# Low halves of 18 weight blocks by adding transfers, and three moves in the order of work, in a decoder layer

## The chip, the cores and the metric

The kernel runs on one core of a Trainium2 chip, as one launch. The metric is device time in microseconds, a median over runs. The core has a matrix engine (PE, with PEld for its weight loads), a vector engine (DVE), an activation engine (ACT), a general engine (POOL), and SyncE (SP), which only issues transfers. Each engine runs its own list of instructions in order and waits on semaphores. ACT and DVE can read the matrix engine's accumulators. Transfers (DMAs) are issued by SP, and by POOL where a transfer adds to what lies at its destination.

## The reference, cut to what matters

One layer of a hybrid decoder, width 1024, 512 tokens, all in float32:

```python
u = rmsnorm(h)
a_glu, q, k, v, r, g_low, gate_a, gate_b = split(u @ w_in)
c = conv31(a_glu[:, :1024] * sigmoid(a_glu[:, 1024:]))
y_conv = silu(layernorm(c)) @ w_conv_out
y_gla = (headnorm(gla_chunked(q, k, v, g_low)) * silu(r)) @ w_gla_out
h = h + (sigmoid(gate_a) * y_conv + sigmoid(gate_b) * y_gla) @ w_o
z = conv3(rmsnorm(h) @ w_ffn_up)            # 1024 -> 2 x 2816
h = h + (silu(z[:, :2816]) * z[:, 2816:]) @ w_ffn_down
return rmsnorm(h)
```

The change touches the layer norm of the convolution branch, the gates, and the channel mixer (`w_ffn_up`, called the up projection, and the product that follows it).

## The kernel before, in words

**Three matmuls for one.** A float32 product is made from parts: every operand is split into a high part, the value rounded to a shorter format, and a low part, what the rounding left over. `mm3` (L444 to L450) then issues three matmuls for one product: low times high, high times low, high times high. In `col_tile` the weight is the stationary operand; its 128x1024 block gives one tile of 128 output channels for 512 tokens, which are 8 x 3 matmuls of 512 columns. The first of each three (L448) reads the weight's low part, so a block can't begin before its low part is there.

**Getting a weight block.** The list `order` holds all blocks in the order of use. `load` lets SP fetch the next 512 KB block into one of four `raw` buffers; `split_weight` (L343 to L392) makes its two parts in one of four `whi` and one of four `wlo` buffers: ACT copies the block into the rounded format (L385), and DVE subtracts that copy from the block (L390). `weight` (used at the start of each block) calls `split_weight` two blocks ahead (`LOOK = 2`). Blocks named in the set `ADDED` (L43) go another way: ACT writes the negated, rounded copy into the low buffer (L387), and then POOL issues a transfer that fetches the block from memory a second time and adds it there (L388). DVE has no part in it. Before the change 16 blocks do so: six of `w_glu`, two of `w_v`, eight of `w_r`.

**Seven products for eight.** Some pairs of output tiles are made together by `two_tiles` with seven quarter products in place of eight (Winograd's form). Such a pair takes two raw blocks and a third buffer for sums that POOL makes of them (`two_sums`, L327): three additions at step `x1` and one at `x3`. The steps `x1`, `x3`, `x2`, `x4` use 256-column matmuls. `put` (L1171) copies an accumulator out on ACT, and `combine` (L1174) works on DVE; the step `x3` adds into the accumulator that `put` has to copy first.

**The merge.** `pair_7` runs such pairs for the gates, with half tiles of `w_gla` or `w_conv` behind each of the four steps. After the last step of a pair ACT takes the sigmoid of both tiles (L1255). Between the blocks, `fill` hands out pieces of side chains by shares: `norm_chain` (L897) is the layer norm of the convolution. Its `ln_center` squares the eight channel tiles and DVE adds the squares (L866); `ln_var` (L868) calls `token_sums` (L834), where PE sums over channels with one-column matmuls (L837); POOL takes the root, and `spread` (L844) brings it back. The order of instructions on each engine is set when the program is built, by a planner that works with costs of its own; `tc.keep_in_program_order` and `tc.issue_after` bind it.

**The up projection.** `up_plan` lists the work of three groups of channel tiles (`GROUPS`). Channel tile f has two blocks, f and 22 + f (`FT + f`). Plain tiles (f = 0, 2, 1, 3, 4, 5, 8 in the first group, 9, 20, 12 in the second, 13, 16, 17, 19 in the third) are `col_tile` blocks; the others are made in sevens. From the second half of the first group on, a unit weaves one plain tile (blocks a and b) into the steps of one pair, in one of three kinds:

- "opens" (tiles 9 and 13): a, x1, a, x3, b, x2, b, x4, b
- the middle kind (tiles 5, 20, 16, 17): x1, a, x3, a, x2, b, x4, b
- "closes" (tiles 8 and 12): x1, a, x3, a, x2, a, x4, and then all of b

`ffn_conv` (L1472) works on a finished tile: one ACT instruction (L1475) and two taps on DVE (L1477). `value` adds the silu (L1482). `second_of_pair` (L1508) makes the operands for the down projection; at L1647 it may be held behind the split of an `x3`. The down projection (`seven`) follows each group; its blocks are also completed by transfers that POOL issues (L317, L300).

Of the kernel before, what the change touches and what calls it, by code (L numbers as in the profile page):

```python
# [15 lines left out]
ALU = mybir.AluOpType  # L16

P = 128
D = 1024
T = 512  # L20
# [8 lines left out]
FT = FF // P  # L29
# [14 lines left out]
ADDED = {("w_glu", 2 * k) for k in range(2, KT)} | {("w_r", m) for m in range(KT)}  # L44
ADDED |= {("w_v", KT // 2 + j) for j in (0, 1)}
RATE = 5.0
WARM = (7, 3, 2)
MID = 4
EARLY = 2
PADS = (416, 2016, 768)  # L50
# [25 lines left out]
def trunk_layer(ctx: ExitStack, tc: tile.TileContext, a: dict, out: bass.AP):  # L76
    nc = tc.nc
# [26 lines left out]
    def heap(dt=F32):  # L104
        return hp.tile([P, T], dt, tag="h", name=nm("h"))
# [13 lines left out]
    def mm_bank():  # L119
        return ps.tile([P, T], F32, tag="mm", name=nm("mm"), bufs=5)  # L120

    def ax_bank():
        return ps.tile([P, T], F32, tag="ax", name=nm("ax"), bufs=3)
# [10 lines left out]
    ones = cp.tile([P, P], F32, name="ones")  # L134
# [264 lines left out]
    def third_ahead():  # L399

        n = used[0] + LOOK
        if n == len(ready) < len(order) and order[n][0] == "two" and order[n][1][-1] == "x3":
            split_weight()
            return two_low[0]
# [59 lines left out]
    def row_half(name, j0, n, acts, nk, done, tok_inner, middle=None):  # L464
# [19 lines left out]
        else:  # L484
            ws = [weight(name, j0 + k, 0) for k in range(nk // 2)]
            for t in range(NT):
                acc = mm_bank()
                for k in range(nk):
                    if middle and k == MID:
                        middle(t)  # L490
# [61 lines left out]
    start = tc.manual_schedule(engines=START)  # L552
# [13 lines left out]
    def warm(n):  # L566
        for _ in range(n):
            nc.tensor.matmul(idle[:, :P], ones, ones, start=True, stop=True)
# [3 lines left out]
    def transposed(x, g):  # L572
        tr = ax_bank()
        for k in range(4):
            c = (g * 4 + k) * P
            nc.tensor.transpose(tr[:, k * P : (k + 1) * P], x[:, c : c + P], ident)
        return tr
# [31 lines left out]
    def early_gain(t, g):  # L609
        xg[t, g] = with_gain(xg[t, g], g)  # L610
        eu[t, g] = [by_four(heap(F32R)) for _ in range(2)]
# [43 lines left out]
    def by_parts(acc, t, ks, parts=(HH, HL, LH)):  # L655

        for wi, ai in parts:
            for k in ks:
                act = eu[t, k // 4][ai][:, k % 4, :] if t < EARLY else acts1[k][ai][:, t * P : (t + 1) * P]
                j = slice((k % 2) * T, (k % 2 + 1) * T)  # L660
                first, last = k == 0 and (wi, ai) == HH, k == KT - 1 and (wi, ai) == LH
                nc.tensor.matmul(acc, act, ready[k // 2][wi][:, j], start=first, stop=last)  # L662

    accs = [mm_bank() for _ in range(EARLY)]
    warm(WARM[0])
    xg[0, 0] = transposed(xs[0], 0)
# [9 lines left out]
    highs[1]()  # L676
    warm(WARM[1])
    lows[0]()
# [5 lines left out]
    by_parts(accs[0], 0, (0, 1), (HL, LH))  # L684
    warm(WARM[2])
    early_gain(1, 0)
# [41 lines left out]
    acc = mm_bank()  # L728
# [7 lines left out]
    acc = mm_bank()  # L736
# [74 lines left out]
    for k in range(KT):  # L811
# [4 lines left out]
        c = heap()  # L816
# [17 lines left out]
    def token_sums(s):  # L834
        b = ax_bank()
        for t in range(NT):
            nc.tensor.matmul(b[:, t : t + 1], s[:, t * P : (t + 1) * P], ones[:, 0:1], start=True, stop=True)  # L837
        return b[:, :NT]

    def spread(v):  # L840
# [18 lines left out]
    def ln_center(k):  # L859
        nc.vector.tensor_tensor(conv[k], stat["mean"], conv[k], ALU.add)  # L860
        sq = btmp()
        nc.scalar.activation(sq, conv[k], AF.Square)
        if k == 0:
            stat["sq"] = sq
        else:
            nc.vector.tensor_tensor(stat["sq"], stat["sq"], sq, ALU.add)  # L866
# [30 lines left out]
    def norm_chain():  # L897
        chain = [(RATE, ln_parts)]
        chain.append((0, ln_mean))
        chain.extend((2, lambda k=k: ln_center(k)) for k in range(KT))  # L900
        chain[-1] = (RATE, chain[-1][1])
        chain.append((2.5, lambda: None))
        chain.append((RATE, ln_var))
        chain.append((2.5, lambda: None))
        chain.append((0, ln_rstd))
        chain.extend((2.5, lambda k=k: ln_out(k)) for k in range(KT))
        return chain
# [17 lines left out]
    for k in range(KT):  # L925
        s = slice(k * P, (k + 1) * P)
# [323 lines left out]
    part = [None] * KT  # L1250
    gas = {}

    def sigmoid(m, acc):
        g = heap()
        nc.scalar.activation(g, acc, AF.Sigmoid)  # L1255
        return g
# [25 lines left out]
    half_of = [range(KT // 2), range(KT // 2, KT)]  # L1282
    open_tiles = {}

    def pair_7(n):
        (name, p, q), behind = MERGE[n], BEHIND[n]
        unit = two_tiles(name, p, q, lambda: merge_acts, mm_bank)
        if behind[0][0] == "w_conv":
            while chains:
                fill(1)  # L1290
        for j in range(4):
            while urgent and j and len(urgent) > (5 if j == 1 else 0):
                urgent.pop(0)[1]()
            done = next(unit)
            if j == 3:
                third_ahead()
                for m, c in zip((p, q), done):
                    (part if name == "w_gb" else gas)[m] = sigmoid(m, c)
            for proj, m, half in behind[j : j + 1]:
                open_tiles[proj, m] = tile_of(proj, m, half_of[half], open_tiles.get((proj, m)))  # L1300

# [170 lines left out]
    def ffn_conv(acc, m):  # L1472
        z = tmp()
        w = [pp[:, PP_FW + m * FW + j : PP_FW + m * FW + j + 1] for j in range(FW)]
        nc.scalar.activation(z, acc, AF.Identity, bias=pp[:, PP_FB + m : PP_FB + m + 1], scale=w[2])  # L1475
        for j, s in ((1, 1), (0, 2)):
            nc.vector.scalar_tensor_tensor(z[:, s:], acc[:, : T - s], w[j], z[:, s:], ALU.mult, ALU.add)  # L1477
        return z

    def value(i, acc):  # L1480
        za = ffn_conv(acc, i)
# [113 lines left out]

    gain3 = None
    banks, values, units = {}, {}, {}
    third = None
    for gi, pairs in enumerate(GROUPS):
        acts = []  # L1600
        if gi == 0:

            ws = [weight("w_up", j, 0) for i in pairs[0] for j in (i, FT + i)]
            accs = [mm_bank() for _ in ws]
            for j, lo in [(j, lo) for lo in (0, H) for j in range(3)]:
                late = {(1, 0): (KT - 1, 2), (2, 0): (MID, 3)}.get((j, lo))
                at = {late[0]: lambda t=late[1]: to_channels(normed[t], u2, t)} if late else {}
                col_tile(ws[j], acts2, accs[j], lo, lo + H, at)
            col_tile(ws[3], acts2, accs[3])
            p, q = pairs[0]  # L1610
            w = first_gated(p, value(p, accs[0]), accs[1])
            found = first_of_pair(w)
            up_acts, sums = ffn_sums()
            s1_n2, of_s1, s4, of_n2, of_s4, n3, of_n3 = sums
            sums = [s1_n2, of_n2 + of_s1, s4 + n3, of_n3 + of_s4]

            def some_sums():
                for _, work in sums.pop(0) if sums else ():
                    work()

            some_sums()
            acts.append(second_of_pair(q, value(q, accs[2]), accs[3], w, found))
            some_sums()
        else:
            found = first_of_pair(w)
        for what, i, *rest in up_plan(gi):
            if what == "tile":
                if 0 in rest[0]:
                    banks[i] = (weight("w_up", i), mm_bank())
                wt, acc = banks[i]  # L1630
                col_tile(wt, acts2, acc, ks=rest[0])
                if KT - 1 in rest[0] and i < FT:
                    values[i] = value(i, acc)
            if what == "part":
                if rest[0] == "x1":
                    units[i] = two_tiles("w_up", i, FT + i, lambda: up_acts, ax_bank)
                done = next(units[i])
                if done:
                    values[i] = value(i, done[0])
                    banks[FT + i] = (None, done[1])  # L1640
                    third = third_ahead()
            if what == "first":
                w = first_gated(i, values.pop(i), banks.pop(FT + i)[1])
                if any(i in pair for pair in pairs):
                    found = first_of_pair(w)
            if what == "second":
                with tc.issue_after(third.ins) if third else ExitStack():  # L1647
                    acts.append(second_of_pair(i, values.pop(i), banks.pop(FT + i)[1], w, found))
                third = None
            if what in ("first", "second"):  # L1650
                some_sums()
        if gi < len(GROUPS) - 1:
            seven("w_down", pairs, acts, lambda t, n, c: None)
        else:
            gain3 = load_gain("final_g")
            seven("w_down", pairs, acts, last_complete, last_at, True)
# [90 lines left out]
```

## Time and profile before

| | before |
|---|---|
| median of 3 runs | 831.78 us (830.68 to 832.02) |
| profiled execution, its own time | 834.48 us |
| its span, first to last instruction | 832.8 us |
| granted clock of PE, mean | 0.993 |
| PE busy | 819.7 us |
| DVE busy | 717.5 us |
| ACT busy | 450.1 us |
| POOL busy | 149.4 us |

Rows of the timeline read: start, duration, engine, line, operation, output <- inputs, shape, count, and in brackets the engine's idle time before it and what ended it. Rows of the waits read: engine, tile and line that waited, what it waited for, total, times, longest. Rows of the windows: the stretch, its length, busy time of PE, PEld, DVE, ACT and POOL with counts, PE's granted clock, the share of the DMA engines, GB/s. Matmuls overlap, so a row's duration is longer than the distance to the next one. A DMA issue's "us to landing" runs from its issue to the last byte's semaphore.

### The profile page before, as it was taken

The page shows a single profiled execution, that of the slowest core. Times are in us where ns is not written, and L with a number is a line of the kernel's source. Part 1 is how long each engine was busy: PE and PEld are TensorE (multiplying, and loading weights), DVE is VectorE, ACT ScalarE, POOL GpSimd, SP SyncE. Part 2 cuts the span into 40 slices and gives each one's busy share as a digit, 9 for nine tenths or more (in the row PEclk, how much of TensorE's full clock was granted, in tenths as well). Part 3 has the DMA queues.
Part 4 walks back from the last instruction along what each step waited for, and adds up shares of the span by engine and source line. Part 5 has one row for each costly group of instructions (what it writes and reads, how often), then busy time and mean ns, then how long its engine had stood idle before and what let it go on. Part 6 is the DMA issues. An engine that isn't in the chain of part 4 may idle for free.

```text
span 832.8 us, 11561 instructions
## 1 busy us (share of the span) xinstructions
PE 819.7 (98%) x4325; PEld 707.6 (85%) x4325; DVE 717.5 (86%) x1161; ACT 450.1 (54%) x666; POOL 149.4 (18%) x133
## 2 busy tenths in 40 slices
PE   8999999999999999899999999999999999999996
PEld 6888888888888889889988898899889988899885
DVE  5689999998989599685778889979984999789996
ACT  5744447656563446494444546556444664456654
POOL 1000010001100213335000200221133301513012
PEclk9999999999999999899999999999999999999999
DMA  7355672563433113223458633046743356324762
GB/s 289 112 123 149 151 185 98 128 152 101 105 100 109 43 50 103 92 87 102 160 144 228 177 102 102 26 136 172 145 130 102 130 146 141 129 84 157 189 128 102
DMA packets 30616, 106.27 MB, mean 128 GB/s; under 512 B 3464, under 2 KB 3600, under 8 KB 30560
## 3 DMA queue, kind: packets, MB, share of 16 engines
q1 hardware_dynamic: 24800, 85.35, 30.4%
q0 software_dynamic: 5760, 20.19, 14.5%
q8 instruction: 34, 0.56, 0.3%
q14 instruction: 22, 0.18, 0.1%
HBM read 103.42 MB, written 2.10 MB: 127 GB/s over the span
## 4 chain that ended last, share of the span: by engine, by line
PE 87%; DVE 8%; issue 2%; ACT 1%; DMA 1%; SPq 0%; POOL 0%; POOLq 0%; ACTq 0%; DVEq 0%
PE mm L448 25%; PE mm L449 25%; PE mm L450 25%; PE ax L450 2%; PE ax L448 2%; PE ax L449 2%; PE mm L662 2%; DVE wlo L356 1%; DMA pp<-in_pp_dram 1%; PE ax L1062 1%; DVE btmp L866 1%; DVE tmpq L1129 1%; DVE wlo L390 1%; PE ax L1064 1%; PE ax L1043 1%
## 5 line engine op out<-in xcount | busy, mean ns | idle before, releaser
L448 PE MATMUL mm<-uh,wlo 128*128 128x512 f32 (+1 forms) x672 | 244.5, 364 | 0.0
L449 PE MATMUL mm<-ul,whi 128*128 128x512 f32 (+1 forms) x672 | 242.3, 361 | 0.0
L450 PE MATMUL mm<-uh,whi 128*128 128x512 f32 (+1 forms) x672 | 241.9, 360 | 0.0
L450 PEld LDWEIGHTS mm<-uh,whi 128*128 128x128 f32 x672 | 126.7, 189 | 19.4
L448 PEld LDWEIGHTS mm<-uh,wlo 128*128 128x128 f32 x672 | 127.0, 189 | 19.1 <-DVE tmp L1174 0.2
L449 PEld LDWEIGHTS mm<-ul,whi 128*128 128x128 f32 x672 | 127.0, 189 | 18.7
L385 ACT CAST whi<-raw 128x1024 fp32r<-128x1024 f32 x86 | 89.6, 1046 | 61.6 <-PE mm L450 38.7
L356 DVE TENSOR_TENSOR wlo<-raw,whi 128x1024 fp32r<-128x1024 f32 x80 | 96.9, 1217 | 27.2 <-ACT whi L355 23.0
L327 POOL TENSOR_TENSOR raw<-raw,raw 128x512 f32<-128x512 f32 x42 | 68.2, 1623 | 222.6 <-DVE wlo L356 127.8
L390 DVE TENSOR_TENSOR wlo<-raw,whi 128x1024 fp32r<-128x1024 f32 x70 | 89.1, 1277 | 16.2 <-ACT whi L385 16.0
L355 ACT CAST whi<-raw 128x1024 fp32r<-128x1024 f32 x80 | 76.3, 958 | 37.6 <-PE mm L450 27.9
L783 DVE SCALAR_TENSOR_TENSOR c<-h,pp,c 128x255 f32<-128x255 f32 (+14 forms) x120 | 57.2, 477 | 3.6 <-ACT c L779 3.3
L783 DVE SCALAR_TENSOR_TENSOR c<-aside,btmp,c 128x255 f32<-128x255 f32 (+14 forms) x120 | 57.2, 477 | 2.8 <-ACT c L779 2.7
L783 DVE SCALAR_TENSOR_TENSOR aside<-h,pp,aside 128x255 f32<-128x255 f32 (+6 forms) x112 | 53.4, 477 | 0.0
L355 ACT CAST whi<-kept 128x1024 fp32r<-128x1024 f32 (+1 forms) x32 | 31.8, 996 | 31.1 <-DVE kept L310 14.8
L1477 DVE SCALAR_TENSOR_TENSOR tmp<-mm,pp,tmp 128x511 f32<-128x511 f32 (+1 forms) x56 | 41.5, 744 | 4.0 <-ACT tmp L1475 3.9
L356 DVE TENSOR_TENSOR wlo<-kept,whi 128x1024 fp32r<-128x1024 f32 (+1 forms) x32 | 37.9, 1186 | 4.3 <-ACT whi L355 4.3
L1171 ACT COPY tmp<-mm 128x256 f32<-128x256 f32 x48 | 17.7, 368 | 34.0 <-PE mm L450 33.5
L1394 DVE TENSOR_TENSOR hres<-hres,mm 128x512 f32<-128x512 f32 (+1 forms) x49 | 32.4, 672 | 3.3 <-PE mm L450 2.0
L1475 ACT ACTIVATE tmp<-mm,pp 128x512 f32<-128x512 f32 x28 | 21.7, 774 | 18.8 <-PE mm L450 18.6
L387 ACT ACTIVATE wlo<-raw 128x1024 fp32r<-128x1024 f32 x16 | 16.8, 1059 | 22.1 <-PE mm L448 22.1
L1477 DVE SCALAR_TENSOR_TENSOR tmp<-tmp,pp,tmp 128x511 f32<-128x511 f32 (+1 forms) x32 | 27.1, 905 | 0.1
(350 smaller groups left out, 1792.3 us busy)
## 6 DMA issues: line engine op xcount, KB each, us to landing
raw<-in_w_up_dram SPq DMA_DIRECT2D x44, 512.0 KB, 3.5
raw<-in_w_glu_dram SPq DMA_DIRECT2D x16, 512.0 KB, 4.8
raw<-in_w_down_dram SPq DMA_DIRECT2D x15, 512.0 KB, 3.9
kept<-in_w_down_dram POOLq DMA_DIRECT2D x10, 512.0 KB, 6.5
raw<-in_w_v_dram SPq DMA_DIRECT2D x8, 512.0 KB, 5.7
raw<-in_w_qk_dram SPq DMA_DIRECT2D x8, 512.0 KB, 3.4
raw<-in_w_r_dram SPq DMA_DIRECT2D x8, 512.0 KB, 4.5
wlo<-in_w_r_dram POOLq DMA_DIRECT2D x8, 512.0 KB, 8.0
```

What stands on the lines that cost most here:

```text
L327: work = nc.gpsimd.tensor_tensor(out, x, y, ALU.add)
L355: nc.scalar.copy(hi, raw)
L356: two_low[:] = [nc.vector.tensor_tensor(lo, raw, hi.bitcast(F32), ALU.subtract)]
L385: nc.scalar.copy(hi, raw)
L390: pace[0] = nc.vector.tensor_tensor(lo, raw, hi.bitcast(F32), ALU.subtract)
L448: nc.tensor.matmul(acc, ll, rh, start=first, stop=False, **kw)
L449: nc.tensor.matmul(acc, lh, rl, start=False, stop=False, **kw)
L450: nc.tensor.matmul(acc, lh, rh, start=False, stop=last, **kw)
L783: nc.vector.scalar_tensor_tensor(out[:, j:], x[:, : half_t - j], w, out[:, j:], ALU.mult, ALU.add)
L1394: done = nc.vector.tensor_tensor(hres[t, n][:, c], hres[t, n][:, c], acc[:, c], op)
L1475: nc.scalar.activation(z, acc, AF.Identity, bias=pp[:, PP_FB + m : PP_FB + m + 1], scale=w[2])
L1477: nc.vector.scalar_tensor_tensor(z[:, s:], acc[:, : T - s], w[j], z[:, s:], ALU.mult, ALU.add)
```

## The change

Four things are changed. (1) The set `ADDED` gets both blocks of the tiles 1, 3, 4, 5, 8, 20, 12, 16 and 17 of the up projection, 18 blocks: for each, the subtraction on DVE is replaced by a negated copy on ACT and an adding transfer on POOL's queue. (2) The token sums keep their place in the program's order, and the chain's shares are changed so that `ln_var` comes later: on PE the eight passes of L837 move behind a half step of the pair and a half tile of `w_gla`, 30 matmuls. (3) In `pair_7` the sigmoids of the first three pairs are taken only after the next pair's first step. (4) `second_of_pair` is also held behind the last tap of `value`, so that both taps of the value tile come ahead of the other tile's.

```diff
+ADDED |= {("w_up", m) for f in (1, 3, 4, 5, 8, 20, 12, 16, 17) for m in (f, FT + f)}
...
-            nc.tensor.matmul(b[:, t : t + 1], s[:, t * P : (t + 1) * P], ones[:, 0:1], start=True, stop=True)
+            product = nc.tensor.matmul(b[:, t : t + 1], s[:, t * P : (t + 1) * P], ones[:, 0:1], start=True, stop=True)
+            tc.keep_in_program_order(product)
...
         chain.extend((2, lambda k=k: ln_center(k)) for k in range(KT))
-        chain[-1] = (RATE, chain[-1][1])
-        chain.append((2.5, lambda: None))
+        chain += [(2.5, lambda: None)] * 4
         chain.append((RATE, ln_var))
...
+    complete_pairs = []
+
     def pair_7(n):
...
             done = next(unit)
+            if j == 0 or n >= 3:
+
+                while complete_pairs:
+                    complete_pairs.pop(0)()
             if j == 3:
                 third_ahead()
-                for m, c in zip((p, q), done):
-                    (part if name == "w_gb" else gas)[m] = sigmoid(m, c)
+
+                def sigmoids(done=done):
+                    for m, c in zip((p, q), done):
+                        (part if name == "w_gb" else gas)[m] = sigmoid(m, c)
+
+                complete_pairs.append(sigmoids)
+                if n >= 3:
+                    complete_pairs.pop()()
...
         for j, s in ((1, 1), (0, 2)):
-            nc.vector.scalar_tensor_tensor(z[:, s:], acc[:, : T - s], w[j], z[:, s:], ALU.mult, ALU.add)
+            taps_at[:] = [
+                nc.vector.scalar_tensor_tensor(z[:, s:], acc[:, : T - s], w[j], z[:, s:], ALU.mult, ALU.add)
+            ]
...
-    third = None
+    third = []
...
-                    third = third_ahead()
+                    third = [taps_at[0], third_ahead()]
...
-                with tc.issue_after(third.ins) if third else ExitStack():
+                with ExitStack() as order_of:
+                    for ins in third:
+                        if ins:
+                            order_of.enter_context(tc.issue_after(ins.ins))
                     acts.append(second_of_pair(i, values.pop(i), banks.pop(FT + i)[1], w, found))
-                third = None
+                third = []
```

More of the change, by code (lines that the diff above doesn't have):

```diff
@@ L1476, in ffn_conv @@
         for j, s in ((1, 1), (0, 2)):
-            nc.vector.scalar_tensor_tensor(z[:, s:], acc[:, : T - s], w[j], z[:, s:], ALU.mult, ALU.add)
+            taps_at[:] = [
+                nc.vector.scalar_tensor_tensor(z[:, s:], acc[:, : T - s], w[j], z[:, s:], ALU.mult, ALU.add)
+            ]
         return z
+    taps_at = []
     def value(i, acc):
```

## The prediction

> **What bounds the kernel now.** I read the page's sums first, then the chain, PE's waits and windows, and at last the single rows around each edit.
>
> ```profile
> span 832.8 us, 11561 instructions
> PE 819.7 (98%) x4325; PEld 707.6 (85%) x4325; DVE 717.5 (86%) x1161; ACT 450.1 (54%) x666; POOL 149.4 (18%) x133
> PE 87%; DVE 8%; issue 2%; ACT 1%; DMA 1%; SPq 0%; POOL 0%; POOLq 0%; ACTq 0%; DVEq 0%
> 490.00:580.00 90.00, 90.00 (x531) 80.04 (x529) 82.81 (x107) 51.94 (x73) 13.38 (x9) 1.00 0.32 101
> 620.00:680.00 60.00, 59.47 (x381) 53.92 (x380) 47.66 (x63) 33.01 (x49) 15.55 (x10) 1.00 0.35 116
> 713.00:775.00 62.00, 62.00 (x393) 56.30 (x392) 50.47 (x66) 34.17 (x51) 19.45 (x11) 1.00 0.40 136
> ```
>
> The matrix engine is the bound: 98% busy, 87% of the chain. The last three rows are windows over the three groups of the up projection, where the 18 blocks lie: PE is busy for 90.00 of 90, 59.47 of 60 and 62.00 of 62 us, at a granted clock of 1.00. So relief of DVE can win next to nothing there, and each microsecond for which a block's low part is late is lost whole. What the change can win lies at PE's few stops:
>
> ```profile
> PE ax L837 <- DVE btmp L866: 2.1, 1, 2.1
> PE mm L448 <- ACT tmp L1171: 1.1, 2, 0.6
> 334.36 0.28 PE L450 MATMUL mm<-sumsq,whi 128*128 128x256 f32 x1
> 336.73 1.50 PE L837 MATMUL ax<-ones,btmp 128*128 128x1 f32 x8 [2.10 <-DVE btmp L866]
> 338.09 0.56 PE L448 MATMUL mm<-sumsq,wlo 128*128 128x256 f32 x1
> 337.00:344.00 7.00, 7.00 (x30) 6.61 (x30) 1.62 (x4) 1.04 (x1) 2.91 (x3) 0.51 0.01 2
> 372.68 0.39 PE L448 MATMUL mm<-xq,wlo 128*128 128x256 f32 x1 [0.55 <-ACT tmp L1171]
> 668.90 0.39 PE L448 MATMUL mm<-xq,wlo 128*128 128x256 f32 x1 [0.53 <-ACT tmp L1171]
> ```
>
> PE waits 2.10 us for the last square (L866), does its eight thin passes, and then runs 7 us at a granted clock of 0.51; two waits of half a microsecond follow.
>
> **Token sums.** Thirty matmuls go ahead of L837. At 0.12 us for a 256-column one (334.36 against its neighbours) and 0.23 for a 512-column one, a half step of the pair (18) and a half tile (12) make 4.9 us. PE comes to L837 at about 339.2, and the squares were there by 336.6: the wait goes, 2.10 us. With it goes the stretch from 334.6 to 338.1 without large matmuls, after which the clock was halved; 7.0 x (1 - 0.51) = 3.4 us more. Next on this chain is `spread` (L844):
>
> ```profile
> 338.26 0.16 DVE L870 TENSOR_SCALAR mean<-ax 128x4 f32<-128x4 f32 x1 [1.68 <-PE ax L837]
> 338.90 1.01 POOL L500 TENSOR_TENSOR rstd<-mean,mhalf 128x4 f32<-128x4 f32 x1
> 350.01 1.05 PE L844 MATMUL ax<-ident,rstd 128*128 128x128 f32 x8
> ```
>
> It stands at 350.01 with no wait, and moved up by the 5.5 us it comes at 344.5. The passes, begun at 339.2, take 1.4 us (336.73 to 338.09), and the root is done 1.8 us behind them (338.90 + 1.01), at 342.4: still not late, by 2 us. Gain 5.5.
>
> **Sigmoids and taps.** The sigmoids of a pair go behind the next pair's first step, so the copy (L1171) that PE waits for at 372.68 stands ahead of them on ACT: I take 0.5 of the 0.55. For the taps, the 0.53 at 668.90 could go as well, but a11's copy is also put behind new work of ACT (below); I count nothing. Bounds 0 and 1.1. Gains together 6.0 us.
>
> **The 18 blocks.** Each takes one subtraction from DVE and adds one negation on ACT, one issue on POOL and 512 KB of traffic:
>
> ```profile
> L390 DVE TENSOR_TENSOR wlo<-raw,whi 128x1024 fp32r<-128x1024 f32 x70 | 89.1, 1277 | 16.2 <-ACT whi L385 16.0
> L387 ACT ACTIVATE wlo<-raw 128x1024 fp32r<-128x1024 f32 x16 | 16.8, 1059 | 22.1 <-PE mm L448 22.1
> L388 POOL DMA_DIRECT2D wlo<-in_w_r_dram x8: 844/870/924, 147.8 to 237.0; - x8
> DMA to landing us min/median/max: 5.4/7.9/10.9
> 56.76 1.07 ACT L387 ACTIVATE wlo<-raw 128x1024 fp32r<-128x1024 f32 x1 [3.45 <-PE mm L448]
> 58.13 0.87 POOL L388 DMA_DIRECT2D wlo<-in_w_glu_dram  x1 [9.82 <-ACT wlo L387]
> 58.41 0.80 SPq L257 DMA_DIRECT2D raw<-in_w_glu_dram  x2
> raw<-in_w_up_dram SPq DMA_DIRECT2D x44, 512.0 KB, 3.5
> ```
>
> DVE loses 18 x 1.28 = 23 us, ACT gains 18 x 1.06 = 19 us (10 blocks in the first window: 51.9 to 62.5 of 90), POOL 18 x 0.87 = 16 us. None of the three is full, so by load this costs nothing. The price is the time until the low part is there. Before, it was one subtraction behind the copy. Now it is the negation, 1.06, the step to POOL's issue (56.76 + 1.07 to 58.13, 0.30), and the landing, for which I take L388's median 7.9: together 9.3 us, with 6.8 and 12.3 by its least and greatest. I take the median, as the next raw load is issued within a microsecond of the adding one (58.41 behind 58.13), and that will be so again: the negation frees the raw buffer.
>
> In the Trainium skill, "DMA: Bandwidth & Descriptors", section "Anatomy of one DMA — SWDGE (gpsimd) path", a transfer issued by POOL is fitted as 2.0 us plus its bytes over 436 GB/s. By that 512 KB would land after 3.2 us, an estimate, with no stall left at the tight blocks and a sum of 825.8; the least of L388's landings, 5.4, is well over it, so the trace doesn't agree.
>
> Most of the 18 have the time: the blocks of tiles 1, 3, 4, 5 and a8 are split two whole blocks ahead, more than 9.3 us before their use (3 by little: 0 to 0.9), and b20, b16, b17, b5 have steps of a pair between. The tight ones, with the copy's start and the first matmul that reads the low part (a and b are a tile's two blocks):
>
> ```profile
> 571.57 1.05 ACT L385 CAST whi<-raw 128x1024 fp32r<-128x1024 f32 x1
> 577.70 0.40 PE L448 MATMUL mm<-uh,wlo 128*128 128x512 f32 x1
> 638.25 1.05 ACT L385 CAST whi<-raw 128x1024 fp32r<-128x1024 f32 x1 [3.75 <-PE ax L450]
> 645.13 0.40 PE L448 MATMUL mm<-uh,wlo 128*128 128x512 f32 x1
> 673.55 1.05 ACT L385 CAST whi<-raw 128x1024 fp32r<-128x1024 f32 x1
> 679.62 0.40 PE L448 MATMUL mm<-uh,wlo 128*128 128x512 f32 x1
> 730.68 1.05 ACT L385 CAST whi<-raw 128x1024 fp32r<-128x1024 f32 x1 [3.75 <-PE ax L450]
> 737.56 0.40 PE L448 MATMUL mm<-uh,wlo 128*128 128x512 f32 x1
> 746.55 1.22 DVE L390 TENSOR_TENSOR wlo<-raw,whi 128x1024 fp32r<-128x1024 f32 x1
> 748.28 0.75 DVE L1477 SCALAR_TENSOR_TENSOR tmp<-mm,pp,tmp 128x511 f32<-128x511 f32 x1
> 748.94 0.69 DVE L356 TENSOR_TENSOR wlo<-raw,whi 128x512 fp32r<-128x512 f32 x1
> 749.76 3.53 POOL L327 TENSOR_TENSOR raw<-raw,raw 128x512 f32<-128x512 f32 x2 [11.86 <-DVE wlo L356]
> 753.26 2.27 POOL L327 TENSOR_TENSOR raw<-raw 128x512 f32<-128x512 f32 x1
> 758.58 0.40 PE L448 MATMUL mm<-uh,wlo 128*128 128x512 f32 x1
> ```
>
> - b8: its negation is put behind the copy, so 571.57 + 1.05 + 9.3 = 581.9 against 577.70: PE stops for 4.2 us (1.7 by the least landing, 7.2 by the greatest).
> - b12, the same place in the second group: 673.55 + 10.3 = 683.9 against 679.62, 4.2 (1.7 to 7.2). What a12 loses (as a17, below) is within this: the copy waits on work of DVE that runs on meanwhile.
> - a20 and a16: the buffer comes free only when PE has left it (3.75 us of waiting before the copy), and the negation stands ahead of the copy: 638.25 + 9.3 = 647.5 against 645.13, 2.4 (0 to 5.4); likewise 730.68 against 737.56, 2.4. The copies of accumulators behind them on ACT come some 2 us later; these stalls hide that, and it costs 1.2 each without them.
> - a17: its issue stands on POOL behind three sums that end at 755.5. They wait on DVE for x4's low part (748.94), which comes some 1.9 us earlier, as b16's subtraction (746.55, 1.22) and a tap (748.28, 0.75) are no longer ahead of it. Issue at 753.6, landing at 759.0 to 761.5, against 758.58: 1.6 (0.4 to 2.9).
>
> Stalls: 2 x 4.2 + 2 x 2.4 + 1.6 = 14.8 us.
>
> **The clock.** A stretch of some 3.5 us without large matmuls (334.6 to 338.1) halved the clock for 7 us; waits of 0.55 us didn't. A stall of 4.2 us is longer than that stretch, one of 2.4 shorter. I charge 3.4 us once, for b8; b12's 4.2 is split by a12. The Trainium skill, "TensorE: Matmul & The Clock Gate", "Part 1: The HAM clock gate", says the clock falls after an idle window of about 3.4 us that runs freely; by it 4.2 may trip and 2.4 can't, the sum taken here. Had the bare wait of 2.10 us done it, each of the four stalls would pay, which is the first rival. The trace alone doesn't part the two, as the wait and the thin passes adjoin.
>
> **Sum.** 14.8 + 3.4 - 6.0 = +12.2 us. The profiled execution took 834.48 us itself (832.8 of span and 1.7 around it), 2.7 above the median of the runs, 831.78; it becomes 846.7, and the median 844.0.
>
> **Rivals.**
> 1. Every stall of 2.1 us or more halves the clock: b12, a20 and a16 pay too, 3 x 3.4 = 10.2 more: 854.2. For it: the dip at 337 began right behind a wait of 2.10. Against: thin passes prolonged that. Chance 0.18.
> 2. Faster: the adding transfers land like the quickest, 5.4 us, because the up projection's windows leave the DMA engines two thirds free (0.32 to 0.40 busy). The stalls are then 1.7, 1.7 and 0.4, none long enough for the clock: 3.8 - 6.0 = -2.2, 829.6. It turns at a mean landing of about 5.9. Against: the median 7.9. Chance 0.17.
> 3. They land like a plain load of 512 KB, 3.5 us: no stall, 825.8. No L388 row does. Chance 0.05.
> 4. The moved token sums do not do what they should: another wait or the thin passes halve the clock there still, and the 5.5 isn't won: 849.5. Chance 0.05.
> 5. Gain and loss meet near 831.8 (landings of about 6). Chance 0.05.
>
> **How the numbers follow.** The forecast, 844.0, has 0.50; by landings of 6.8 to 8.2 and the clock's dip at none to two places its own range is 836 to 850. What a measurement can tell from no change is about 0.2%, 1.7 us. Faster: rivals 2 and 3, 0.22; same: rival 5, 0.05; slower: the forecast, 1 and 4, 0.73. From 827.5, which takes in rival 2 with its 0.5 us left over at 372 and 668 and the landing's scatter, to 859, which adds a landing 1 us longer at five blocks to rival 1.
>
> **What would show it.** Right: no wait of L837 and a clock near 1 at 337; L388 on `w_up` x18 with a landing near 7.9; waits of PE at L450 (the moved L448) for POOL's transfers at b8, b12, a20, a16 and a17 of 4, 4 (with a12), 2, 2 and 1.6 us; windows after them at about half the clock once. Wrong: landings near 5.5; copies or negations that start earlier than 571.57, 638.25 and their like stand to their uses; or dips behind the short stalls.

## The result, and the profile after

| | before | after |
|---|---|---|
| median of 5 runs | 831.36 us | 845.68 us (844.39 to 848.45) |
| ratio | | 1.0175 (95% interval 1.0156 to 1.0194) |
| span of the profiled execution | 832.8 us | 844.0 us |
| PE waiting for an adding transfer of `w_up` | none | 11.3 us at 7 places |

The change costs 14.3 us by the medians, where 12.2 were forecast. The lines of the changed kernel stand 2 or 3 lower in the code up to L1282 and 4 to 18 lower behind it, so the old L448 is L450, L387 is L389, L388 is L390. Of its page: the busy times, the chain by engine, the new groups, and the new transfers.

```profile
span 844.0 us, 11589 instructions
PE 822.2 (97%) x4325; PEld 708.1 (84%) x4325; DVE 695.6 (82%) x1143; ACT 466.8 (55%) x684; POOL 163.0 (19%) x151
PE 84%; DMA 7%; issue 4%; DVE 3%; ACT 1%; POOL 1%; SPq 0%; POOLq 0%; ACTq 0%
L389 ACT ACTIVATE wlo<-raw 128x1024 fp32r<-128x1024 f32 x34 | 35.9, 1058 | 36.7 <-PE mm L450 26.3
raw<-in_w_up_dram SPq DMA_DIRECT2D x44, 512.0 KB, 5.0
wlo<-in_w_up_dram POOLq DMA_DIRECT2D x18, 512.0 KB, 7.8
```

DVE is 22 us less busy and ACT 17 more, and neither moves the end. What is new is DMA with 7% of the chain: it was 1%. The adding transfers land 7.8 us after their issue, as the 7.9 taken from L388. The plain loads beside them now take 5.0 us in place of 3.5. Next PE's waits, first summed, then row by row:

```profile
PE mm L450 <- DMA wlo<-in_w_up_dram: 11.3, 7, 3.9
PE mm L450 <- ACT tmp L1173: 0.3, 1, 0.3
513.65 0.47 PE L450 MATMUL mm<-uh,wlo 128*128 128x512 f32 x1 [1.08 <-DMA wlo<-in_w_up_dram]
576.70 0.80 PE L450 MATMUL mm<-uh,wlo 128*128 128x512 f32 x1 [3.92 <-DMA wlo<-in_w_up_dram]
648.48 0.50 PE L450 MATMUL mm<-uh,wlo 128*128 128x512 f32 x1 [1.35 <-DMA wlo<-in_w_up_dram]
670.03 0.50 PE L450 MATMUL mm<-uh,wlo 128*128 128x512 f32 x1 [0.28 <-DMA wlo<-in_w_up_dram]
684.86 0.77 PE L450 MATMUL mm<-uh,wlo 128*128 128x512 f32 x1 [1.89 <-DMA wlo<-in_w_up_dram]
745.97 0.50 PE L450 MATMUL mm<-uh,wlo 128*128 128x512 f32 x1 [1.33 <-DMA wlo<-in_w_up_dram]
779.99 0.50 PE L450 MATMUL mm<-uh,wlo 128*128 128x512 f32 x1 [1.49 <-DMA wlo<-in_w_up_dram]
338.63 0.95 PE L839 MATMUL ax<-ones,btmp 128*128 128x1 f32 x8
```

They are, in this order, a of tile 3, b8, a20, a12, b12, a16 and b17. Their transfers landed 9.2, 7.9, 7.1, 8.0, 5.9, 7.1 and 10.5 us after their issues. The last row is the token sums, which no longer wait. The way of b8 in single rows, copy, negation, issue and first use:

```profile
566.30 1.05 ACT L387 CAST whi<-raw 128x1024 fp32r<-128x1024 f32 x1
567.25 1.05 ACT L389 ACTIVATE wlo<-raw 128x1024 fp32r<-128x1024 f32 x1
568.72 0.88 POOL L390 DMA_DIRECT2D wlo<-in_w_up_dram  x1 [10.32 <-ACT wlo L389]
```

From the issue to the use it unblocks (576.70) are 8.0 us. The granted clock stands in windows of the changed kernel:

```profile
572.50:575.80 3.30, 0.28 (x3) 0.07 (x1) 3.26 (x4) 3.30 (x6) 1.35 (x2) 0.98 1.01 187
575.80:582.40 6.60, 5.70 (x13) 4.46 (x14) 3.74 (x6) 1.08 (x2) 0.38 (x1) 0.50 0.94 215
682.80:684.80 2.00, 0.17 (x2) 0.00 (x0) 2.00 (x4) 1.86 (x4) 1.49 (x2) 1.00 0.73 117
684.90:688.30 3.40, 3.40 (x8) 2.75 (x9) 3.33 (x5) 1.99 (x4) 0.12 (x1) 0.50 0.93 172
330.00:345.00 15.00, 15.00 (x106) 13.97 (x105) 12.18 (x15) 7.94 (x13) 7.34 (x5) 1.00 0.34 118
```

The clock is halved from the last microsecond of b8's wait on, over the 6.6 us of the second window, and behind b12's wait for 3.4. Of the first of these stretches 0.9 us is still waiting; the work in the rest and in the second is 5.7 and 3.4 us long and would take half of that: 2.85 and 1.7 us lost. Around the token sums it is 1.00.

### The profile page after: what moved, and what is told of

It is laid out like the page before. It is cut to its first block, busy times and chain, and to the rows that moved or that the text cites. A ratio compares the mean times of both kernels' runs of the same rounds, so it can differ in the third digit from the quotient of the medians.

```text
span 844.0 us, 11589 instructions
## 1 busy us (share of the span) xinstructions
PE 822.2 (97%) x4325; PEld 708.1 (84%) x4325; DVE 695.6 (82%) x1143; ACT 466.8 (55%) x684; POOL 163.0 (19%) x151
## 4 chain that ended last, share of the span: by engine, by line
PE 84%; DMA 7%; issue 4%; DVE 3%; ACT 1%; POOL 1%; SPq 0%; POOLq 0%; ACTq 0%
PE mm L450 24%; PE mm L451 24%; PE mm L452 24%; DMA wlo<-in_w_up_dram 6%; PE mm L664 2%; PE ax L450 1%; PE ax L452 1%; PE ax L451 1%; DMA pp<-in_pp_dram 1%; PE ax L1064 1%; DVE tmp L1492 1%; DVE wlo L358 1%; PE ax L1066 1%; PE ax L1045 1%; POOL raw L329 1%
## 5 line engine op out<-in xcount | busy, mean ns | idle before, releaser
L450 PE MATMUL mm<-uh,wlo 128*128 128x512 f32 (+1 forms) x672 | 247.3, 368 | 11.4 <-DMA wlo<-in_w_up_dram 11.3
L450 PEld LDWEIGHTS mm<-uh,wlo 128*128 128x128 f32 x672 | 128.0, 190 | 32.4 <-DMA wlo<-in_w_up_dram 11.5
L358 DVE TENSOR_TENSOR wlo<-raw,whi 128x1024 fp32r<-128x1024 f32 x80 | 94.3, 1185 | 44.6 <-ACT whi L357 36.9
L387 ACT CAST whi<-raw 128x1024 fp32r<-128x1024 f32 x86 | 89.4, 1044 | 47.5 <-PE mm L452 33.1
L329 POOL TENSOR_TENSOR raw<-raw,raw 128x512 f32<-128x512 f32 x42 | 65.9, 1570 | 156.0 <-DVE wlo L358 109.4
L392 DVE TENSOR_TENSOR wlo<-raw,whi 128x1024 fp32r<-128x1024 f32 x52 | 66.3, 1281 | 14.3 <-ACT whi L387 14.3
L389 ACT ACTIVATE wlo<-raw 128x1024 fp32r<-128x1024 f32 x34 | 35.9, 1058 | 36.7 <-PE mm L450 26.3
L390 POOL DMA_DIRECT2D wlo<-in_w_up_dram x18 | 15.6, 869 | 74.6 <-ACT wlo L389 66.1
```

The source lines that it names most:

```text
L329: work = nc.gpsimd.tensor_tensor(out, x, y, ALU.add)
L358: two_low[:] = [nc.vector.tensor_tensor(lo, raw, hi.bitcast(F32), ALU.subtract)]
L387: nc.scalar.copy(hi, raw)
L389: pace[0] = nc.scalar.mul(lo, raw, -1.0)
L392: pace[0] = nc.vector.tensor_tensor(lo, raw, hi.bitcast(F32), ALU.subtract)
L450: nc.tensor.matmul(acc, ll, rh, start=first, stop=False, **kw)
```

## The experiments

All times are medians, and ratios are against the kernel before as it ran on the same chip. It ran on these chips at 830.67 to 831.36 us, so a difference between two runs of different chips is good to some 0.7 us.

### The orders without the blocks, and the blocks without the orders

`order_only` takes the 18 blocks out of the changed kernel, `added_only` puts only them into the kernel before:

```diff
-ADDED |= {("w_up", m) for f in (1, 3, 4, 5, 8, 20, 12, 16, 17) for m in (f, FT + f)}
```

> The changed kernel without the 18 adding blocks: token sums, sigmoids and taps in the new order alone. Theory (the blocks' landings are the whole loss): no wait for a transfer is left and the gain of 6.0 us stands alone, 831.4 - 6.0 = 825.4. If the halved clock at 337 of before is not in every execution, only the waits are won in those, 2.6 us: 828.8. Rival (the new order costs): 831.4 or above.

> The kernel before with the 18 adding blocks alone. Theory: the changed kernel's loss at its seven waits and two stretches of half clock, 17 us, with nothing won: about 849 to 852, 3 to 6 above the changed kernel. Rival (the loss comes from the new order): near 831.

Measured: `order_only` 829.85 us beside 830.67, ratio 0.9991 (0.9982 to 1.0000); `added_only` 853.05, ratio 1.0268 (1.0245 to 1.0290). So the loss is the blocks': 845.68 - 829.85 = 15.8 us on top of the new order, 22.4 on top of the old one, a little more than expected. Of the 6.6 us that the old order pays more for the same blocks, PE's waits for their transfers hold 4.9, 16.2 us at 8 places in `added_only` in place of 11.3 at 7:

```profile
PE mm L449 <- DMA wlo<-in_w_up_dram: 16.2, 8, 4.4
```

The largest differences are at b12 (3.77 for 1.89), b17 (2.55 for 1.49) and b20 (1.16 for none). Why these blocks come later in the old order stays open.

But the orders won only 0.8 us, not 6.0 and not the 2.6 of the cautious reading either. PE's waits in `order_only`:

```profile
PE mm L449 <- ACT tmp L1172: 1.1, 4, 0.3
PE mm L449 <- DVE tmp L1175: 0.9, 1, 0.9
```

The copy that PE waited for twice (0.55 and 0.53) is now waited for four times, 1.1 us together as before, and at 372 a wait for `combine` on DVE has come in place of the one for ACT. That led to the three runs that follow.

### The kernel before once more, the token sums alone, and the taps undone

`before_again` is the unchanged kernel under a second profile. `token_only` is it with the token sums moved:

```diff
+            tc.keep_in_program_order(product)
...
-        chain[-1] = (RATE, chain[-1][1])
-        chain.append((2.5, lambda: None))
+        chain += [(2.5, lambda: None)] * 4
```

`token_sig` is `order_only` with the old order of the taps:

```diff
-                    third = [taps_at[0], third_ahead()]
+                    third = [third_ahead()]
```

> The kernel before, unchanged, profiled a second time. If the halved clock behind the token sums belongs to this wait, the window 337 to 344 again runs at about 0.5. If it is a matter of how the wait falls against the clock's own windows, it may be shorter or missing, with the span some 1.7 or 3.4 us below 832.8.

> The kernel before with the token sums moved, nothing else. Theory now: the wait of 2.10 us goes in every execution, the stretch of half clock (3.4) was there in the profiled one and in few others: 2.1 to 2.6 below before, 828.3. The forecast's reading (2.10 and 3.4 each time): 825.2. Rival (the move wins nothing): 830.7.

> Token sums and sigmoids in the new order, the taps in the old one. Theory: the new order of the taps puts a copy of an accumulator late at four places (4 x 0.53 us of PE in place of one), so without it the time is 1.6 below that of all three orders together (829.85): 828.3. Rival (the taps cost nothing): 829.9.

`before_again` took 830.11 us with a span of 828.4. Its wait for the squares, and the window that ran at half clock in the first profile:

```profile
335.50 0.69 PE L837 MATMUL ax<-ones,btmp 128*128 128x1 f32 x5 [0.88 <-DVE btmp L866]
337.00:344.00 7.00, 7.00 (x50) 6.51 (x50) 3.99 (x5) 3.11 (x4) 3.06 (x3) 1.00 0.25 74
```

The wait is 0.88 us, not 2.10, and the clock stays at 1.00. The two prices on which most of the forecast's gain rested are 1.2 + 3.4 = 4.6 us dearer in the profile that was read than in this one, and the spans differ by 4.4. `token_only` came to 828.85 us beside 830.85, ratio 0.9982 (0.9973 to 0.9991): 2.0 us won, not 5.5. Of the 21 executions of the kernel before beside it, five have a mean clock of 0.995, and none of the 11 of `token_only` is under 0.997, which fits a dip of the clock that only some executions have. `token_sig` came to 828.58, ratio 0.9976 (0.9967 to 0.9985). So the sigmoids add nothing that can be told (0.3), and the new taps cost 829.85 - 828.58 = 1.3 us. In `token_sig` one wait for the copy is left, of 0.5 us, where `order_only` has four of 1.1 together: these waits show 0.6 of the 1.3. The theory had reckoned with 4 x 0.53, so that it met the time is in part luck. Both versions are faster than either kernel of the change.

### Which blocks

`no_closers` lets b8 and b12 subtract again; `closers_only` adds these two alone; `loose_only` has 8 blocks that PE did not wait for. In the last two the line takes the place of the one that adds all 18:

```diff
+ADDED -= {("w_up", FT + f) for f in (8, 12)}                     # no_closers
...
+ADDED |= {("w_up", FT + f) for f in (8, 12)}                     # closers_only
...
+ADDED |= {("w_up", m) for f in (1, 4, 5) for m in (f, FT + f)} | {("w_up", 8), ("w_up", FT + 20)}   # loose_only
```

> The changed kernel with the b blocks of tiles 8 and 12 subtracting again, 16 adding blocks left. Theory (late landings at single places): the waits of 3.92 and 1.89 and the two stretches at half clock go, some 10.6 us: 845.7 - 10.6 = 835.1. Rival (18 more transfers, copies and issues slow everything a little): two eighteenths of the 14 to 20 us, 844.

> The three new orders and only two adding blocks, the b blocks of tiles 8 and 12. Theory: their waits (3.92 and 1.89 in the changed kernel, b12's up to 4 where nothing stalled before it) and a stretch of half clock behind each (2.9 and 1.9): 10.6 to 13 above the orders alone (829.85), 840 to 843, with two transfers of eighteen. Rival (loss by the number of transfers): 831.6.

> The new order and 8 adding blocks that PE did not wait for in the changed kernel: both of tiles 1, 4 and 5, a of 8 and b of 20. Theory: as the new order alone, within 1 us. Rival (the traffic, ACT's or POOL's work costs): eight eighteenths of 14 to 20 us above it, 6 to 9 us.

| | us | ratio to before | above `order_only` |
|---|---|---|---|
| `no_closers` | 835.92 | 1.0069 (1.0050 to 1.0088) | 6.1 |
| `closers_only` | 839.35 | 1.0093 (1.0066 to 1.0121) | 9.5 |
| `loose_only` | 830.37 | 0.9993 (0.9981 to 1.0006) | 0.5 |

`no_closers` and `loose_only` came where the theory had them. The loss is not spread over the transfers. Two of the 18 make 9.5 of 15.8 us, the other sixteen 6.1, and these two numbers add up to 15.6. Eight transfers with time to spare cost 0.5 us, which can't be told from nothing; what DVE is spared wins nothing either. `closers_only` stayed 0.65 us under its range in the median; its four executions spread from 836.26 to 840.78, at mean clocks of 0.997 to 0.991. The profiled one, 840.35, lies in the range, and in it b12 waited for 2.59 us, not for 4:

```profile
575.63 0.80 PE L450 MATMUL mm<-uh,wlo 128*128 128x512 f32 x1 [4.02 <-DMA wlo<-in_w_up_dram]
683.44 0.50 PE L450 MATMUL mm<-uh,wlo 128*128 128x512 f32 x1 [2.59 <-DMA wlo<-in_w_up_dram]
```

### What makes the landing long

`plain_pool` leaves the addition out of the 18 transfers and keeps their queue and size. `neg_first` puts the negation ahead of the copy and binds both in that order, for all 18; `neg_first_closers` for b8 and b12 only:

```diff
-                nc.gpsimd.dma_start(lo, a[name][spec], accum_op=ALU.add)
+                nc.gpsimd.dma_start(lo, a[name][spec])            # plain_pool, w_up only
...
+            if name == "w_up" and (name, spec) in ADDED:           # neg_first
+                pace[0] = nc.scalar.mul(lo, raw, -1.0)
+                tc.keep_in_program_order(pace[0])
+                nc.gpsimd.dma_start(lo, a[name][spec], accum_op=ALU.add)
+                tc.keep_in_program_order(nc.scalar.copy(hi, raw))
...
```

> The changed kernel, its 18 transfers on POOL's queue without the addition (they overwrite the negated copy, so the low parts are not the low parts; times alone count). If the addition at the destination makes the landing long, it falls from 7.8 towards the 3.5 of a plain load, the waits go and the time is near 831. If it is the queue and the loads beside it, landings stay at 7 or more and the time at 845.

> The changed kernel with the negation ahead of the copy for all 18 blocks (it stood behind the copy for b8, b12 and four more). Theory: transfers of b8 and b12 start 1.0 us sooner, so the waits of 3.92 and 1.89 shrink to 2.9 and 0.9 and the second stretch of half clock goes: 2 to 4 us below 845.7, 842 to 844. Rival (the landing is set by traffic, not by the start): 845.7.

> The changed kernel with the negation ahead of the copy for b8 and b12 alone; on ACT nothing else changes its place. Theory: their transfers start 1.0 us sooner, the waits shrink from 3.92 and 1.89 to some 3.0 and 1.0, and the second stretch of half clock may go: 1.8 to 3.7 us below the changed kernel's 845.7, 842 to 844. Rival (the landing is set by the loads beside it): 845.7.

`plain_pool` took 833.95 us, ratio 1.0039 (1.0024 to 1.0054). Its transfers' landings, and PE's waits for them:

```profile
DMA to landing us min/median/max: 3.6/4.9/8.0
PE mm L453 <- DMA wlo<-in_w_up_dram: 1.6, 2, 1.2
```

Without the addition the median falls from 7.8 to 4.9 us and 11.7 of the 15.8 us of loss are gone. So it is the addition more than the queue: in this same run the plain loads of `w_up` that SP issues take 4.5 us in the median, and the transfers of `w_r` and `w_glu`, which still add, 7.8. The slowest are those issued among other transfers. In `plain_pool` that is the one at 760.11, with four loads beside it (8.0 us). In the changed kernel two adding ones, issued at 506.23 and 508.18 behind a third at 504.32, landed after 10.9 and 11.6 us, the third after 9.2.

`neg_first` came to 856.3 us, ratio 1.0305 (1.0285 to 1.0324), where 842 to 844 was expected. The binding moved more than the two instructions at b8: the first of the 18 blocks was negated at 500.01, where the changed kernel has 490.26, and waits of 3.99, 1.73 and 3.03 us came up between 500 and 552 that the changed kernel doesn't have:

```profile
507.00 0.80 PE L458 MATMUL mm<-uh,wlo 128*128 128x512 f32 x1 [3.99 <-DMA wlo<-in_w_up_dram]
534.29 0.47 PE L458 MATMUL mm<-uh,wlo 128*128 128x512 f32 x1 [1.73 <-DVE tmp L1500]
551.34 0.50 PE L458 MATMUL mm<-uh,wlo 128*128 128x512 f32 x1 [3.03 <-DMA wlo<-in_w_up_dram]
```

In that run other moves hide the answer, so `neg_first_closers` swaps nothing but those two pairs. It took 845.16 us, ratio 1.0180 (1.0157 to 1.0203): the 0.5 us to the changed kernel lie within both intervals, and the theory's 1.8 to 3.7 did not come in the median. The profiled execution is the fastest of the four, 842.95, and lies in the theory's range; its rows:

```profile
576.79 0.63 PE L458 MATMUL mm<-uh,wlo 128*128 128x512 f32 x1 [3.12 <-DMA wlo<-in_w_up_dram]
684.03 0.50 PE L458 MATMUL mm<-uh,wlo 128*128 128x512 f32 x1 [2.05 <-DMA wlo<-in_w_up_dram]
```

b8's wait shrank nearly as worked out, 3.92 to 3.12. b12's did not, 1.89 to 2.05. I read that as the raw load beside it. In the changed kernel the load goes out 0.4 us ahead of the adding transfer, and 6.0 us lie between the issue and the use it unblocks (684.86):

```profile
678.50 0.33 SPq L298 DMA_DIRECT2D raw<-in_w_down_dram  x1
678.88 0.89 POOL L390 DMA_DIRECT2D wlo<-in_w_up_dram  x1 [10.32 <-ACT wlo L389]
```

In `neg_first_closers` it goes out 0.6 us behind it, since the copy now frees the raw buffer last, and 7.1 us pass:

```profile
676.92 0.89 POOL L390 DMA_DIRECT2D wlo<-in_w_up_dram  x1 [9.37 <-ACT wlo L388]
677.48 0.33 SPq L298 DMA_DIRECT2D raw<-in_w_down_dram  x1
```

The load alone was not moved, so its part in this is argued and not shown.

## Why the prediction was right, and where it was not

The forecast of 844.0 us met 845.68, but by two errors that partly cancel: the cost was put at 18.2 and is 15.8, the gain at 6.0 and is 0.8. The mechanism of the loss was right; that the sum came so close is in part luck.

- **What bounds the kernel.** Right. `loose_only` shows that relief of DVE wins nothing, and `closers_only` that single late low parts are the loss.
- **Token sums, 5.5.** The mechanism was right: no wait, no half clock, and `spread` (now L847) isn't late. The size was wrong, 2.0 us in `token_only`. The sum took both the wait of 2.10 and the 3.4 of the clock from one execution that was itself 2.7 us above the median, noted that distance and did not ask where it lay. It lay here: in `before_again` the wait is 0.88 and the clock stays up.
- **Sigmoids, 0.5.** Not won, and the step that failed is that the wait at 372 was taken for one of its own. `token_only`, with the sigmoids in their old order, has a single wait for the copy left, the one behind 660; the moved token sums alone had removed the one at 372. With the sigmoids moved too, in `token_sig`, PE waits there for `combine` on DVE:

```profile
PE mm L448 <- ACT tmp L1171: 0.5, 1, 0.5
373.16 0.39 PE L449 MATMUL mm<-uh,wlo 128*128 128x256 f32 x1 [1.00 <-DVE tmp L1175]
```

  The first row is `token_only`, the second `token_sig`. The gain is 0.3, within the error; why the wait of 1.00 us doesn't show in the time stays open. In the changed kernel neither wait stands at 372.
- **Taps, 0, with bounds of 0 and 1.1 together with the sigmoids.** Wrong in sign: -1.3. The bounds had no loss in them, although the same paragraph said that copies are put later on ACT.
- **The landing, 7.9.** Right in the median, 7.8. The "DMA: Bandwidth & Descriptors" page of the Trainium skill, in its section on the path of POOL's transfers, would have had 3.2, an estimate; the least of the plain ones here is 3.6 and the median of the adding ones 7.8, so the fit fails most for the addition.
- **The places.** b8: 4.2 forecast, 3.92. a20 and a16: 2.4 each, 1.35 and 1.33. b12 with a12: 4.2, 1.89 + 0.28. a17: 1.6, no wait; 7.6 us lay between its issue (759.54) and its use (767.13), where the forecast had 5.0. For a17 alone the sum took the middle of two landings, 5.4 and 7.9. On the other side two blocks were called covered and weren't: a of tile 3 (1.08, "0 to 0.9") and b17 (1.49). For b17 the cover was reckoned with the median, and its transfer was issued among four loads:

```profile
769.40 0.87 POOL L390 DMA_DIRECT2D wlo<-in_w_up_dram  x1 [3.30 <-ACT wlo L389]
768.47 0.33 SPq L259 DMA_DIRECT2D raw<-in_w_up_dram  x1
768.85 0.90 SPq L298 DMA_DIRECT2D kept<-in_w_down_dram  x2
769.96 0.33 SPq L298 DMA_DIRECT2D raw<-in_w_down_dram  x1
```

  It landed only after 10.5 us. One landing for all blocks was the weak step: at the seven places it was 5.9 (b12) to 10.5 us (b17), and together 14.8 of waiting were forecast and 11.3 measured.
- **The clock, 3.4 once.** The first rival (all four stalls) didn't come, and b8's did; but b12's shorter one of 1.89 tripped it too, for half as long. 2.85 + 1.7 = 4.6 us in the profiled execution. The rule behind the term, that a stall must be longer than the 3.5 us seen before the change, was wrong; what the traces show in its place stands at the end.
- **The faster rivals** needed mean landings below 5.9. `plain_pool`, with a median of 4.9, is that case made real: it is 4.1 us above the orders alone and, as the orders win so little, still slower than before. The sum of the second rival also left out the 1.2 us each that the prediction itself sets for a20 and a16 where they don't stall; with them it is +0.2, no gain at all. No row gives that 1.2. In `plain_pool` PE waits 2.3 us for copies, in place of 1.1 in `order_only`.

## What to carry to other kernels

When a transfer takes the place of an instruction, compare block by block the time from its issue to the first use with its landing under the traffic of that place, not with one median; the two blocks with the least lead paid more than half of the price. Before a wait and a clock dip of one profile are booked as a gain, look whether that execution is slower than the median, and by how much. Where an edit moves copies on an engine that releases accumulators, put a loss into its bounds.

## What the runs showed of the hardware

**An addition at the destination lengthens the landing.** 512 KB from POOL's queue landed after 3.6 us at least and 4.9 in the median without it. With it, over all 34 adding transfers of the changed kernel:

```profile
DMA to landing us min/median/max: 5.3/7.8/11.6
```

**The clock drops behind shorter stalls than I had charged, and not behind every one.** PE's waits of these traces, the most that fell into one stretch of the grid that is explained below, and the clock right after. Where the token sums stand behind the wait, the thin passes count as idle, as no large matmul runs in them:

| kernel | wait, us | in one stretch, us | clock after |
|---|---|---|---|
| `before_again`, token sums | 0.88 | 1.51 | 1.0 |
| `added_only`, token sums | 1.07 | 1.96 | 0.50 for 3.4 us |
| `no_closers` | 1.63 | 1.53 | 1.0 |
| after, b12 | 1.89 | 1.89 | 0.50 for 3.4 us |
| `neg_first_closers`, b12 | 2.05 | 1.21 | 1.0 |
| before, token sums | 2.10 | 2.48 | 0.50 for 6.8 us |
| `closers_only`, b12 | 2.59 | 2.59 | 0.57 over 3.5 us |
| `neg_first`, 551 | 3.03 | 1.80 | 1.0 |
| `neg_first_closers`, b8 | 3.12 | 3.12 | 0.54 over 3.5 us |
| after, b8 | 3.92 | 2.91 | 0.50 for 6.8 us |

Windows of `closers_only` (b12) and of `neg_first_closers` (b12, then b8):

```profile
683.50:687.00 3.50, 3.50 (x9) 2.73 (x10) 3.33 (x5) 1.28 (x2) 0.00 (x0) 0.57 1.00 211
```
```profile
684.00:687.50 3.50, 3.47 (x15) 2.90 (x16) 3.42 (x5) 1.92 (x4) 0.03 (x1) 1.00 0.93 174
576.70:580.20 3.50, 3.41 (x8) 2.63 (x9) 3.33 (x6) 1.07 (x2) 0.37 (x1) 0.54 1.01 187
```

By the length of the wait alone, both outcomes occur between 1.89 and 3.03 us. The dips last 3.41 us or twice that, and the moments at which the clock falls lie on a grid of 3.413 us that doesn't start with the stall: in `added_only` at 336.18, 578.53 and 691.17 (71 and 33 steps apart), in the changed kernel at 575.69 and 684.91 (32 steps), in `neg_first` at 505.17 and 590.50 (25 steps).

With each trace cut along its grid, one rule covers all 13 profiles up to the last 30 us of the kernel. At the end of every stretch of 3.41 us that began at full clock and had 1.89 us or more without large matmuls the clock fell, 11 times in all, and behind none with 1.80 or less did it fall. The two nearest to the border are b12 of the changed kernel and, behind it, the wait at 551 of `neg_first`, which falls into two stretches, with 1.23 and 1.80 us; each is shown with the stretch that follows:

```profile
681.50:684.91 3.41, 1.52 (x14) 1.31 (x12) 3.41 (x5) 3.19 (x5) 1.60 (x2) 1.00 0.79 139
684.91:688.33 3.42, 3.42 (x8) 2.77 (x9) 3.35 (x5) 1.98 (x4) 0.11 (x1) 0.50 0.95 174
549.54:552.95 3.41, 1.61 (x7) 1.35 (x8) 2.12 (x3) 1.33 (x2) 0.00 (x0) 1.00 1.00 354
552.95:556.36 3.41, 3.41 (x23) 3.04 (x22) 0.69 (x1) 1.19 (x2) 0.87 (x1) 1.00 0.64 105
```

A first stretch at half clock without idle time was the only one (6 dips); one with 0.87 us or more of it was followed by a second (5 dips). So a stall of a given length costs clock or not by how it lies on the grid.

The Trainium skill, "TensorE: Matmul & The Clock Gate", "Part 1: The HAM clock gate", has such a free-running window of about 3.4 us and asks for an idle one; the grid agrees with these traces, but a stretch a little over half idle (1.89 of 3.41 us) was enough. Where between 1.80 and 1.89 the border lies, and whether it is the same in other kernels, these runs leave open.
